# The last MLP's pair sums on DVE instead of POOL, and five slots instead of three for the weights of the modulation dot products

## The chip, the cores and the metric

The kernel runs on one core of a Trainium2 chip. The metric is the device time of one execution in microseconds (us). Five engines work side by side, each through its own instructions in order: PE (TensorE, matrix products), DVE (VectorE), ACT (ScalarE), POOL (GpSimd) and SP (SyncE, which here issues all DMA transfers). PE writes to PSUM, in banks of 128 x 512 f32 words; DVE and ACT read PSUM and SBUF, and POOL's instructions in this kernel read SBUF alone.

## The reference

Two layers of a diffusion backbone over 1024 latent tokens and 256 context tokens, 1024 channels wide: a convolution mixer with its MLP, then grouped-query attention with its MLP. Every sub-layer is modulated by vectors that come from a conditioning vector. What the change touches, cut down:

```python
sc = silu(c); scc = silu(c_ctx)
for i in range(2):
    mod_l = split(sc  @ w_mod[i] + b_mod[i], 6)       # 6 vectors of 1024
    mod_c = split(scc @ w_mod[i] + b_mod[i], 6)
    ...                                               # mixer: convolution (i = 0), attention (i = 1)
    hl = modulate(rms_norm(xl, norm2_g[i]), mod_l[3], mod_l[4])
    xl = xl + mod_l[5] * (square(relu(hl @ w_ff1[i])) @ w_ff2[i])     # d_ff = 4096
```

## The kernel before

All products are f32 made of three passes (high part times high, low times high, high times low), so each weight block is first split: ACT copies it to a rounded high part, and POOL or DVE subtracts to get the low part (`unit`, `lower`).

**The modulation vectors of layer 1** (`mods`, L338 to L370) are not made on PE. They are 128 dot products on DVE ("dots", L363): each takes a 128 x 512 block of weights (`rawh`, loaded by SP, L354) and multiplies it with half of silu(c) (`scp`, two PSUM banks written by ACT, L348, from the tile `sc`). They come in three runs (32 for c, 32 for c_ctx, 64 for c), each of which loads `sc` anew. The weights rotate through three slots, borrowed from the idle tiles `ks`, `vt`, `sb`, and a load is requested two dots ahead. The dots are background work: `pump` hands them out between the steps of layer 0's MLP (`mlp`), where each costs `MQ` credits. Their place on DVE, among the MLP's evacuations of PSUM (L439 `hb`, L461 `X`), is then set by a scheduler with its own idea of durations. In the trace they lie between 737 and 990 us.

**The last MLP** (`mlp1`) uses a seven-product scheme (Strassen-Winograd) on blocks. The loop over 16 pairs of hidden blocks (`for j in range(NP)`) makes, per pair, the products of S1 (bank b5), S3 (b7), S2 (b6), S4 (b5 again, added) and A22 (b7 again, added). For the first eight pairs (`pro`) the A11 product was made before and lies in DRAM (`p1d`), so a pair is five products; for the later ones it is seven. `w1_ops` prepares a pair's weights: SP loads `ra` and `rb` (L1343, L1344, three `raw` slots), DVE forms four sums in `work` (L1357 to L1361), ACT and POOL split them (L1350, L1198), and A22 is split by ACT and DVE (L1364, L1365) into the tile with the tag `p1`, which has one slot.

The sums of a pair: ACT copies b5 to p5 (L1409) and b7 to p7 (L1413), POOL adds p5 += p7 (L1416), DVE adds p1 += b6 (L1419), POOL adds p5 += p1 (L1420). `tail` runs one pair later: relu and square of p5 (`hidden`, L1307, L1308, with its store L1309), s12 = b5 + p1 and p1 = b7 + p1 on DVE (L1376, L1377), relu and square on ACT (L1378, L1379; L1307, L1308), the differences t1 (DVE L1384), t2 (POOL L1386), s12 (DVE L1388) and t4 (DVE L1391), each stored to `hd` by SP (L1383). S4 adds into b5, so PE cannot start S4 before the copy L1409 has read the bank. `ff2` then reads `hd`.

Of the kernel before, what the change touches and what calls it, by code (L numbers as in the profile page):

```python
# [14 lines left out]
AF = mybir.ActivationFunctionType  # L15
ALU = mybir.AluOpType
# [4 lines left out]
P = 128  # L21
D = 1024
KT = D // P
# [4 lines left out]
TAPS = 31  # L28
# [34 lines left out]
_off = 0  # L63
for _n, _w in [("n1", 16), ("n2", 16), ("bmod", 96), ("bdw", 8), ("lng", 8), ("lnb", 8), ("taps", 8 * TAPS)]:
    VEC[_n] = (_off, _w)
    _off += _w
# [12 lines left out]

MQ = 0.73  # L80
G3 = [4.2, 4.2, 4.2, 4.2]
# [31 lines left out]
BUFS = {"w8": 5, "raw": 3, "rawm": 1, "xu": 3, "hl": 2, "hb": 1, "tmp": 5, "acc": 3, "sc": 1, "qs": 1, "ks": 1,  # L113
        "vt": 1, "sb": 1, "cc": 1, "m3": 2, "halo": 1, "v4": 1, "r4s": 1, "r4y": 1, "pc": 10, "p1": 1}

# [12 lines left out]
class Kern:  # L128
# [209 lines left out]
    def mods(self, i1, chunks, cond, dst):  # L338
# [12 lines left out]
        def load(i):  # L351
            j, u, z = units[i]
            raw = self.t(("ks", "vt", "sb")[i % 3], [P, 512], "rawh")
            nc.sync.dma_start(out=raw, in_=self.A["wmod1"][j * 8 + u, :, z * 512:z * 512 + 512])  # L354
            return raw
        raws = [load(0), load(1)]
        for i, (j, u, z) in enumerate(units):
            if i + 2 < len(units):
                raws.append(load(i + 2))
            if u == z == 0:  # L360
                part = self.t("mp", [P, 2, 8], "mp")
            raw = raws.pop(0)
            nc.vector.tensor_tensor_reduce(raw, raw, scp[z], 1.0, 0.0, ALU.mult, ALU.add,  # L363
                                           accum_out=part[:, z, u:u + 1])
            yield MQ
            if u == 7 and z:
                nc.vector.tensor_tensor(part[:, 0], part[:, 0], part[:, 1], ALU.add)
                self.mod_done(i1, j, dst, part[:, 0])
                self.mdone.add((i1, cond, j))
                yield 0.2  # L370
# [160 lines left out]
    def conv_block(self, b):  # L531
# [5 lines left out]
        N -= off  # L537
        to, bo = VEC["taps"][0], VEC["bdw"][0]
        vs = None
        for c2 in range(0, KT, 2):  # L540
# [6 lines left out]
            for j in range(TAPS):  # L547
                for z in range(2):
                    ct = c2 + z
                    src = u[:, ct, off + j:off + j + N]  # L550
                    tap = self.vec[:, to + ct * TAPS + j:to + ct * TAPS + j + 1]
                    if j == 0:
# [647 lines left out]
    def mlp1(self, at, pre, r0):  # L1200
# [171 lines left out]
        def tail(j, p1, p5, s11, b5, b7):  # L1372
# [12 lines left out]
            out("T1", t1)  # L1385
            nc.gpsimd.tensor_tensor(t2, p5, t1, ALU.subtract)  # L1386
            out("T2", t2)
# [7 lines left out]
        for j in range(NP):  # L1395
# [3 lines left out]
            p1 = ring[2 * (j % 2)]  # L1399
            if pro:  # L1400
                nc.sync.dma_start(out=p1, in_=self.p1d[:, j])
            else:
                b1 = bank(q, "b1")
# [7 lines left out]
            self.prod(b7, u["S3"], piece("T3"), True)  # L1411
            p7 = self.t("acc", [P, 512], "p7")
            nc.scalar.activation(p7, b7, AF.Copy)  # L1413
            if last:
                tail(*last)
            nc.gpsimd.tensor_tensor(p5, p5, p7, ALU.add)  # L1416
            b6 = bank(q + 3, "b6")
            self.prod(b6, u["S2"], piece("T2"), True)
            nc.vector.tensor_tensor(p1, b6, p1, ALU.add)  # L1419
            nc.gpsimd.tensor_tensor(p5, p5, p1, ALU.add)  # L1420
            s11 = self.t("tmp", [P, 512], "s11")
# [118 lines left out]
    def build(self):  # L1540
# [3 lines left out]
        self.vec = const.tile([P, NVEC], F32, name="vec")  # L1544
        nc.sync.dma_start(out=self.vec, in_=self.A["vec"])
        self.ident = const.tile([P, P], F32, name="ident")
# [29 lines left out]
        self.pp = ctx.enter_context(tc.tile_pool(name="ps", bufs=1, space=PSUM))  # L1576

        self.halo = self.t("halo", [P, KT, HALO], "halo")
        self.hb = self.t("hb", [P, 8 * BW], "hb", F32R)
# [68 lines left out]
```

## Time and profile before

| | us |
|---|---|
| median of three runs (2904.96 to 2914.39) | 2907.84 |
| the profiled execution | 2907.84 |
| its span, first to last instruction | 2905.9 |
| PE busy in the span | 2752.6 (95%) |
| DVE, ACT, POOL busy | 2005.7, 1483.5, 1657.6 |

The span leaves 1.9 us of the execution's time around it. An engine's busy time counts only its computing instructions; a matmul's end is modelled, so a busy PE need not run at its peak. "Idle before, releaser" names the instruction whose end let a waiting engine go on.

### The profile page before, as it was taken

The page shows a single profiled execution, that of the slowest core. Times are in us where ns is not written, and L with a number is a line of the kernel's source. Part 1 is how long each engine was busy: PE and PEld are TensorE (multiplying, and loading weights), DVE is VectorE, ACT ScalarE, POOL GpSimd, SP SyncE. Part 2 cuts the span into 40 slices and gives each one's busy share as a digit, 9 for nine tenths or more (in the row PEclk, how much of TensorE's full clock was granted, in tenths as well). Part 3 has the DMA queues.
Part 4 walks back from the last instruction along what each step waited for, and adds up shares of the span by engine and source line. Part 5 has one row for each costly group of instructions (what it writes and reads, how often), then busy time and mean ns, then how long its engine had stood idle before and what let it go on. Part 6 is the DMA issues. An engine that isn't in the chain of part 4 may idle for free. (4 is left out here: it accounts for less than half of the span.)

```text
span 2905.9 us, 36468 instructions
## 1 busy us (share of the span) xinstructions
PE 2752.6 (95%) x12634; PEld 2314.2 (80%) x12634; DVE 2005.7 (69%) x3268; ACT 1483.5 (51%) x2386; POOL 1657.6 (57%) x1286
## 2 busy tenths in 40 slices
PE   7999999999988999989998899998999889999999
PEld 2778999999888999978886677776667677878887
DVE  3888988988465432456358899976986645458797
ACT  4543554546444354536345577655675544454332
POOL 3777766676565664444434466654666556564332
PEclk9999999999999999999999999999999999999999
DMA  6454433343776634444444411132106555474452
GB/s 240 167 176 153 132 120 109 116 141 119 266 239 202 206 109 160 132 133 129 138 145 142 133 22 23 22 95 65 23 8 208 160 181 170 148 254 174 160 176 103
DMA packets 176584, 406.69 MB, mean 140 GB/s; under 512 B 21328, under 2 KB 64848, under 8 KB 174352
## 3 DMA queue, kind: packets, MB, share of 16 engines
q1 hardware_dynamic: 176400, 404.37, 42.8%
q8 instruction: 99, 1.62, 0.2%
q14 instruction: 85, 0.70, 0.1%
HBM read 343.49 MB, written 60.82 MB: 139 GB/s over the span
## 5 line engine op out<-in xcount | busy, mean ns | idle before, releaser
L210 POOL TENSOR_TENSOR wsp<-raw,wsp 128x512 fp32r<-128x512 f32 x508 | 662.0, 1332 | 411.2 <-ACT wsp L207 370.2
L218 PE MATMUL ps<-h,wsp 128*128 128x432 f32 (+1 forms) x2832 | 575.9, 361 | 5.6 <-ACT h L318 2.3
L218 PEld LDWEIGHTS ps<-h,wsp 128*128 128x128 f32 x2832 | 534.8, 190 | 44.5 <-issue 8.3
L207 ACT ACTIVATE wsp<-raw 128x1024 fp32r<-128x1024 f32 x291 | 306.6, 1057 | 321.9 <-PE ps L218 208.0
L556 DVE SCALAR_TENSOR_TENSOR cv<-u,vec,cv 128x464 f32<-128x464 f32 (+2 forms) x696 | 423.1, 671 | 6.2 <-ACT cv L553 4.8
L218 PE MATMUL ps<-hb,wsp 128*128 128x432 f32 (+1 forms) x1920 | 399.3, 362 | 20.5 <-DVE X L461 12.6
L1083 POOL TENSOR_TENSOR p<-e,p 128x512 fp32r<-128x512 f32 x223 | 307.3, 1390 | 164.0 <-ACT p L1081 99.2
L218 PEld LDWEIGHTS ps<-hb,wsp 128*128 128x128 f32 x1920 | 363.3, 190 | 41.6 <-issue 16.3
L1188 PE MATMUL b<-u 128*128 128x512 f32 x1344 | 305.1, 389 | 1.0 <-DVE sums L1453 1.0
L1188 PEld LDWEIGHTS b<-u 128*128 128x128 f32 x1344 | 252.3, 188 | 53.7 <-issue 1.4
L1076 ACT ACTIVATE e<-sT 128x512 f32<-128x512 f32 x320 | 185.9, 596 | 122.0 <-PE sT L1074 100.6
L1038 DVE TENSOR_REDUCE m<-s 128x1 f32<-128x512 f32 (+1 forms) x336 | 191.9, 590 | 11.3 <-PE s L1036 10.1
L1198 POOL TENSOR_TENSOR u<-tf,u 128x512 fp32r<-128x512 f32 x56 | 101.5, 1833 | 150.3 <-ACT u L1447 136.1
L461 DVE SCALAR_TENSOR_TENSOR X<-ps,m,X 128x432 f32<-128x432 f32 (+2 forms) x144 | 81.3, 587 | 117.9 <-PE ps L218 117.7
L363 DVE CUSTOM_DVE_ANT_0 rawh<-rawh,scp 128x512 f32<-128x512 f32 x128 | 86.5, 685 | 108.2 <-DMA rawh<-in_wmod 101.1
L439 DVE TENSOR_TENSOR hb<-ps,hb 128x432 fp32r<-128x432 f32 (+1 forms) x96 | 57.5, 599 | 115.0 <-ACT ps L438 114.7
L1079 DVE CAST p<-e 128x512 fp32r<-128x512 f32 x160 | 115.5, 722 | 29.8 <-ACT e L1076 25.4
L1188 PE MATMUL b<-T,wsp 128*128 128x512 f32 x576 | 133.2, 389 | 0.0
L210 POOL TENSOR_TENSOR wx<-raw,wx 128x512 fp32r<-128x512 f32 x90 | 115.6, 1307 | 24.9 <-ACT wx L207 24.4
L1090 PE MATMUL O<-p,half 128*128 128x512 f32 x320 | 126.9, 396 | 0.0
L1188 PEld LDWEIGHTS b<-T,wsp 128*128 128x128 f32 x576 | 108.2, 188 | 22.6
L218 PE MATMUL ps<-h,wx 128*128 128x432 f32 (+1 forms) x624 | 125.5, 356 | 0.0
(314 smaller groups left out, 5346.5 us busy)
## 6 DMA issues: line engine op xcount, KB each, us to landing
raw<-in_w SPq DMA_DIRECT2D x232, 512.0 KB, 3.4
raw<-in_pw SPq DMA_DIRECT2D x72, 512.0 KB, 3.5
rawh<-in_wmod SPq DMA_DIRECT2D x128, 256.0 KB, 3.5
tf<-hd SPq DMA_DIRECT2D x56, 512.0 KB, 4.2
raw<-in_qkv SPq DMA_DIRECT2D x36, 512.0 KB, 3.4
rawp<-in_wmod SPq DMA_DIRECT2D x32, 512.0 KB, 4.3
raw<-in_w2s SPq DMA_DIRECT2D x16, 1024.0 KB, 7.0
hd<-t SPq DMA_DIRECT2D x48, 256.0 KB, 3.2
```

The source lines that it names most:

```text
L207: nc.scalar.activation(hi(c, n), raw[:, c * P:(c + n) * P], AF.Copy)
L210: (eng or nc.gpsimd).tensor_tensor(lo(c, n), raw[:, c * P:(c + n) * P], hi(c, n).bitcast(F32), ALU.subtract)
L218: self.nc.tensor.matmul(ps, lhsT=(wh, wl, wh)[t], rhs=(ah, ah, al)[t], start=first and i == t == 0, stop=last and i == n - 1 and t == 2)
L363: nc.vector.tensor_tensor_reduce(raw, raw, scp[z], 1.0, 0.0, ALU.mult, ALU.add, accum_out=part[:, z, u:u + 1])
L556: nc.vector.scalar_tensor_tensor(dst, src, tap, acc[z][:, :N], ALU.mult, ALU.add)
L1038: nc.vector.reduce_max(m3[:, qt, j, c:c + 1], s[:, :w], axis=AX.X)
L1076: nc.scalar.activation(e, s, AF.Exp, scale=0.125)
L1079: nc.vector.tensor_copy(p[:, 0], e)
L1083: (nc.vector if u % lm == lm - 1 else nc.gpsimd).tensor_tensor(p[:, 1], e, p[:, 0].bitcast(F32), ALU.subtract)
L1090: nc.tensor.matmul(O[1], lhsT=self.half, rhs=p[:, 0], start=a, stop=False)
L1188: self.nc.tensor.matmul(ps, lhsT=w[t % 2](k), rhs=(ah, ah, al)[t], start=first and k == t == 0, stop=k == 3 and t == 2, skip_group_check=True)
L1198: eng.tensor_tensor(w[:, 1, i:i + n], src[:, i:i + n], w[:, 0, i:i + n].bitcast(F32), ALU.subtract)
```

## The change

In the last MLP the second sum p5 += p7 is made by DVE straight from the bank b7, so that the copy to p7 goes; p5 += p1 and t2 move from POOL to DVE; the load of the stored product p1 is written after `tail`; the tag `p1` (A22's split) has two slots. In `mods` two more slots are taken from the halves of `sc`, a load is requested three dots ahead, and `MQ` goes from 0.73 to 1.2. The convolution's taps leave the tile `vec` for a tile of their own that is freed after the attention.

```diff
-        ... ("lnb", 8), ("taps", 8 * TAPS)]:
+        ... ("lnb", 8)]:
-MQ = 0.73
+MQ = 1.2
-        "vt": 1, "sb": 1, "cc": 1, "m3": 2, ... "pc": 10, "p1": 1}
+        "vt": 1, "sb": 1, "cc": 1, "taps": 1, "m3": 2, ... "pc": 10, "p1": 2}
...
         def load(i):
             j, u, z = units[i]
-            raw = self.t(("ks", "vt", "sb")[i % 3], [P, 512], "rawh")
+            if i % 5 < 3:
+                raw = self.t(("ks", "vt", "sb")[i % 5], [P, 512], "rawh")
+            else:
+                raw = sc[:, i % 5 * 512 - 1536:i % 5 * 512 - 1024]
             nc.sync.dma_start(out=raw, in_=self.A["wmod1"][j * 8 + u, :, z * 512:z * 512 + 512])
             return raw
-        raws = [load(0), load(1)]
+        raws = [load(i) for i in range(3)]
         for i, (j, u, z) in enumerate(units):
-            if i + 2 < len(units):
-                raws.append(load(i + 2))
+            if i + 3 < len(units):
+                raws.append(load(i + 3))
...
-            nc.gpsimd.tensor_tensor(t2, p5, t1, ALU.subtract)
+            nc.vector.tensor_tensor(t2, p5, t1, ALU.subtract)
...
-            if pro:
-                nc.sync.dma_start(out=p1, in_=self.p1d[:, j])
-            else:
+            if not pro:
                 b1 = bank(q, "b1")
...
-            p7 = self.t("acc", [P, 512], "p7")
-            nc.scalar.activation(p7, b7, AF.Copy)
+            nc.vector.tensor_tensor(p5, b7, p5, ALU.add)
             if last:
                 tail(*last)
-            nc.gpsimd.tensor_tensor(p5, p5, p7, ALU.add)
+            if pro:
+                nc.sync.dma_start(out=p1, in_=self.p1d[:, j])
             b6 = bank(q + 3, "b6")
             self.prod(b6, u["S2"], piece("T2"), True)
             nc.vector.tensor_tensor(p1, b6, p1, ALU.add)
-            nc.gpsimd.tensor_tensor(p5, p5, p1, ALU.add)
+            nc.vector.tensor_tensor(p5, p5, p1, ALU.add)
...
+        self.taps_w = self.t("taps", [P, KT * TAPS], "taps")
+        nc.sync.dma_start(out=self.taps_w, in_=self.A["vec"][:, NVEC:])
```

The lines of the changed kernel stand four lines later in `tail` and `w1_ops` (L1343 is L1347), and two later in the pair loop (L1409 is L1411, L1420 is L1422).

On DVE, one pair of the first eight before, from the first operand sum of the coming pair (names with a number are buffers; `raw` and `work` are as in the text above):

```order
L1357 TENSOR_TENSOR work<-raw 128x512
L1358 TENSOR_TENSOR work<-raw 128x512
L1360 TENSOR_TENSOR work<-work,raw 128x512
L1361 TENSOR_TENSOR work<-raw,work 128x512
L1419 TENSOR_TENSOR work<-b_20572,work 128x512
L1376 TENSOR_TENSOR s_20665<-b_20520,work 128x512
L1384 TENSOR_TENSOR t_20673<-s_20665,s_20587 128x512
L1388 TENSOR_TENSOR s_20665<-work,s_20665 128x512
L1377 TENSOR_TENSOR work<-b_20534,work 128x512
L1365 TENSOR_TENSOR a_20629<-raw,a_20629 128x512
L1391 TENSOR_TENSOR t_20681<-work,t_20674 128x512
```

The same engine and a pair of the first eight, of the changed kernel, from its second row on:

```order
L1362 TENSOR_TENSOR work<-raw 128x512
L1414 TENSOR_TENSOR work<-b_20821,work 128x512
L1364 TENSOR_TENSOR work<-work,raw 128x512
L1365 TENSOR_TENSOR work<-raw,work 128x512
L1421 TENSOR_TENSOR work<-b_20858,work 128x512
L1422 TENSOR_TENSOR work<-work 128x512
L1380 TENSOR_TENSOR s_20949<-b_20807,work 128x512
L1388 TENSOR_TENSOR t_20957<-s_20949,s_20873 128x512
L1381 TENSOR_TENSOR work<-b_20821,work 128x512
L1369 TENSOR_TENSOR a_21026<-raw,a_21026 128x512
L1390 TENSOR_TENSOR t_20958<-work,t_20957 128x512
L1392 TENSOR_TENSOR s_20949<-work,s_20949 128x512
```

Three rows are new: the sum with b7 (L1414) behind the coming pair's first two operand sums, p5 += p1 (L1422) directly behind p1 += b6, and t2 (L1390).

On SP, the same pair before, with the two weight loads `raw` of coming pairs and the stores to `hd` of p5, t1, t2, s12, p1 and t4:

```order
L1343 DMA raw<-in_w 128x1024
L1309 DMA hd<-work 128x512
L1383 DMA hd<-t_20786 128x512
L1383 DMA hd<-t_20787 128x512
L1383 DMA hd<-s_20778 128x512
L1344 DMA raw<-in_w 128x1024
L1309 DMA hd<-work 128x512
L1383 DMA hd<-t_20794 128x512
L1423 DMA s_20813<-hd 128x512
L1401 DMA work<-p1d 128x512
```

And of the changed kernel:

```order
L1347 DMA raw<-in_w 128x1024
L1313 DMA hd<-work 128x512
L1387 DMA hd<-t_20846 128x512
L1348 DMA raw<-in_w 128x1024
L1313 DMA hd<-work 128x512
L1387 DMA hd<-t_20847 128x512
L1387 DMA hd<-s_20838 128x512
L1387 DMA hd<-t_20854 128x512
L1425 DMA s_20873<-hd 128x512
L1418 DMA work<-p1d 128x512
```

The second weight load stood behind the stores of t1, t2 and s12 and now stands directly behind that of t1; the load of the stored product has kept its place in the queue.

On SP, in the first stretch of the dots before: `raw` (L197) are the MLP's weights, `rawh` the dots' weights, and `sc` here is the conditioning vector of the second run.

```order
L197 DMA raw<-in_w 128x1024 x2
L354 DMA rawh<-in_wmod 128x512 x2
L197 DMA raw<-in_w 128x1024
L354 DMA rawh<-in_wmod 128x512 x3
L197 DMA raw<-in_w 128x1024
L354 DMA rawh<-in_wmod 128x512 x3
L342 DMA sc<-in_cctx 128x1024
L354 DMA rawh<-in_wmod 128x512 x7
L197 DMA raw<-in_w 128x1024
```

The same place of the changed kernel, where `sc<-in_wmod` are the dots' weights in the two new slots:

```order
L197 DMA raw<-in_w 128x1024 x2
L358 DMA sc<-in_wmod 128x512 x2
L197 DMA raw<-in_w 128x1024
L358 DMA rawh<-in_wmod 128x512 x3
L197 DMA raw<-in_w 128x1024
L358 DMA sc<-in_wmod 128x512 x2
L358 DMA rawh<-in_wmod 128x512 x3
L358 DMA sc<-in_wmod 128x512 x2
L358 DMA rawh<-in_wmod 128x512 x3
L358 DMA sc<-in_wmod 128x512 x2
L358 DMA rawh<-in_wmod 128x512 x2
L197 DMA raw<-in_w 128x1024
```

Between the last two weight loads of these pieces stood ten loads for dots and the second run's `sc`, and now stand fourteen loads and no `sc`.

Further on in the same queue of the changed kernel, the second run's `sc` comes:

```order
L358 DMA sc<-in_wmod 128x512 x2
L358 DMA rawh<-in_wmod 128x512
L197 DMA raw<-in_w 128x1024
L358 DMA rawh<-in_wmod 128x512
L342 DMA sc<-in_cctx 128x1024
L358 DMA rawh<-in_wmod 128x512
L197 DMA raw<-in_w 128x1024
```

It has moved behind the last two dots of the first run that use `sc` as slots, so it can only be issued when they are done; two of ACT's L348 stand right behind, on ACT ahead of the next evacuation.

## Rows read from the trace of the kernel before

**Rows 1.** The head of the page, and its first part: busy us, share of the span and instructions of each engine.

```profile
span 2905.9 us, 36468 instructions
PE 2752.6 (95%) x12634; PEld 2314.2 (80%) x12634; DVE 2005.7 (69%) x3268; ACT 1483.5 (51%) x2386; POOL 1657.6 (57%) x1286
```

**Rows 2.** Busy time in three stretches: the dots (737 to 990 us), the first eight pairs (2307.97 to 2440.70) and the later eight. Columns: stretch, its length, busy us (instructions) of PE, PEld (weight loads), DVE, ACT and POOL, then the granted TensorE clock as a share of full speed, the DMA engines' busy share, GB/s.

```profile
737.00:990.00 253.00, 227.66 (x1098) 210.78 (x1097) 140.05 (x378) 110.37 (x184) 146.01 (x119) 0.97 0.71 234
2307.97:2440.70 132.73, 117.04 (x481) 93.05 (x480) 64.72 (x84) 59.98 (x90) 83.16 (x61) 0.96 0.55 182
2440.70:2594.00 153.30, 152.47 (x665) 124.59 (x664) 75.44 (x87) 80.73 (x123) 98.24 (x70) 1.00 0.52 170
```

**Rows 3.** Waits of PE between 2290 and 2620 us: what waited, for whom, us in total, times, the longest.

```profile
PE b L1188 <- ACT work L1409: 15.6, 7, 3.2
PE b L1188 <- ACT work L1405: 0.8, 2, 0.6
```

**Rows 4.** PE in order of time in the pair loop (start, us, operation, in brackets the idle time before it and its releaser). The rows with T and x36 are the products of S1, S3 and S2 of one pair; the row with u,wsp is S4.

```profile
2307.97 8.32 PE L1188 MATMUL b<-T,wsp 128*128 128x512 f32 x36
...
2322.13 8.32 PE L1188 MATMUL b<-T,wsp 128*128 128x512 f32 x36
2333.32 4.54 PE L1188 MATMUL b<-u,wsp 128*128 128x512 f32 x12 [2.86 <-ACT work L1409]
...
2440.70 2.88 PE L1188 MATMUL b<-B,wsp 128*128 128x512 f32 x12
```

**Rows 5.** All engines in order of time over one pair of the first eight.

```profile
2323.01 2.63 POOL L1198 TENSOR_TENSOR wsp<-work,wsp 128x512 fp32r<-128x512 f32 x2 [1.73 <-ACT wsp L1350]
2323.16 0.69 DVE L1419 TENSOR_TENSOR work<-b,work 128x512 f32<-128x512 f32 x1
...
2325.60 1.29 POOL L1420 TENSOR_TENSOR work<-work 128x512 f32<-128x512 f32 x1
...
2326.93 0.63 ACT L1307 ACTIVATE work<-work 128x512 f32<-128x512 f32 x1 [2.59 <-POOL work L1420]
...
2329.44 0.69 DVE L1384 TENSOR_TENSOR t<-s,s 128x512 f32<-128x512 f32 x1 [4.81 <-ACT s L1379]
...
2330.21 1.77 POOL L1386 TENSOR_TENSOR t<-work,t 128x512 f32<-128x512 f32 x1 [0.80 <-DVE t L1384]
2330.77 0.68 DVE L1377 TENSOR_TENSOR work<-b,work 128x512 f32<-128x512 f32 x1
...
2332.68 0.58 ACT L1409 ACTIVATE work<-b 128x512 f32<-128x512 f32 x1
...
2332.89 0.40 SPq L1344 DMA_DIRECT2D raw<-in_w  x1
...
2337.80 0.69 DVE L1357 TENSOR_TENSOR work<-raw 128x512 f32<-128x512 f32 x1 [4.24 <-DMA raw<-in_w]
2338.41 0.69 DVE L1358 TENSOR_TENSOR work<-raw 128x512 f32<-128x512 f32 x1
...
2339.13 1.06 ACT L1350 ACTIVATE wsp<-work 128x1024 fp32r<-128x1024 f32 x1 [5.38 <-DVE work L1358]
...
2350.11 0.40 SPq L1344 DMA_DIRECT2D raw<-in_w  x1
```

**Rows 6.** Groups of instructions by line between 2308 and 2600 us, of DVE (two SBUF inputs) and of ACT: busy us and mean ns of one, then idle us before them and releasers.

```profile
L1388 DVE TENSOR_TENSOR s<-work,s 128x512 f32<-128x512 f32 x15 | 20.1, 1340 | 0.2
L1307 ACT ACTIVATE work<-work 128x512 f32<-128x512 f32 x31 | 19.6, 632 | 105.7 <-POOL work L1420 87.0 <-DVE work L1377 18.7
```

**Rows 7.** Waits of PE between 700 and 1050 us.

```profile
PE ps L218 <- DVE X L461: 12.6, 7, 3.5
PE ps L218 <- DVE hb L439: 7.1, 6, 3.0
PE st L253 <- DVE acc L286: 5.6, 1, 5.6
```

**Rows 8.** The tile `rawh`: the dots on DVE (ns min/median/max), what ended DVE's idle time before them (us, times), and the time from a load's issue to its landing.

```profile
L363 DVE CUSTOM_DVE_ANT_0 rawh<-rawh,scp x128: 671/686/691, 737.8 to 990.1; 128x512 f32<-128x512 f32 x128
...
  DMA rawh<-in_wmod: 101.1, 67
...
DMA to landing us min/median/max: 2.5/3.5/7.4
```

**Rows 9.** Moments of the dots' stretch: a dot and the evacuation behind it on DVE, then PE; and PE at half clock behind its longest wait.

```profile
757.48 0.69 DVE L363 CUSTOM_DVE_ANT_0 rawh<-rawh,scp 128x512 f32<-128x512 f32 x1 [1.70 <-DMA rawh<-in_wmod]
...
759.99 0.40 DVE L461 SCALAR_TENSOR_TENSOR X<-ps,m,X 128x176 f32<-128x176 f32 x1
...
760.92 1.41 PE L218 MATMUL ps<-hb,wsp 128*128 128x432 f32 x3 [3.54 <-DVE X L461]
...
875.32 5.31 PE L218 MATMUL ps<-h,wsp 128*128 128x432 f32 x14
```

**Rows 10.** The loads of `sc` between 735 and 990 us (KB each, us from issue to landing), and what ACT waited for before its L348 (us, times).

```profile
sc<-in_cctx SPq DMA_DIRECT2D x1, 512.0 KB, 6.0
sc<-in_c SPq DMA_DIRECT2D x1, 512.0 KB, 4.6
...
  DVE mp L363: 8.9, 3
```

**Rows 11.** SP's second issue after the start.

```profile
1.18 0.42 SPq L632 DMA_DIRECT2D cc<-in_ccol  x1
```

More of the change, by code (lines that the diff above doesn't have):

```diff
@@ L63 @@
 _off = 0
-for _n, _w in [("n1", 16), ("n2", 16), ("bmod", 96), ("bdw", 8), ("lng", 8), ("lnb", 8), ("taps", 8 * TAPS)]:
+for _n, _w in [("n1", 16), ("n2", 16), ("bmod", 96), ("bdw", 8), ("lng", 8), ("lnb", 8)]:
     VEC[_n] = (_off, _w)
@@ L113 @@
 BUFS = {"w8": 5, "raw": 3, "rawm": 1, "xu": 3, "hl": 2, "hb": 1, "tmp": 5, "acc": 3, "sc": 1, "qs": 1, "ks": 1,
-        "vt": 1, "sb": 1, "cc": 1, "m3": 2, "halo": 1, "v4": 1, "r4s": 1, "r4y": 1, "pc": 10, "p1": 1}
+        "vt": 1, "sb": 1, "cc": 1, "taps": 1, "m3": 2, "halo": 1, "v4": 1, "r4s": 1, "r4y": 1, "pc": 10, "p1": 2}
 KEEP = ("w8", "raw", "xu", "tmp", "acc", "v4", "r4s", "r4y")
@@ L537, in conv_block @@
         N -= off
-        to, bo = VEC["taps"][0], VEC["bdw"][0]
+        bo = VEC["bdw"][0]
         vs = None
@@ L550, in conv_block @@
                     src = u[:, ct, off + j:off + j + N]
-                    tap = self.vec[:, to + ct * TAPS + j:to + ct * TAPS + j + 1]
+                    tap = self.taps_w[:, ct * TAPS + j:ct * TAPS + j + 1]
                     if j == 0:
@@ L1544, in build @@
         self.vec = const.tile([P, NVEC], F32, name="vec")
-        nc.sync.dma_start(out=self.vec, in_=self.A["vec"])
+        nc.sync.dma_start(out=self.vec, in_=self.A["vec"][:, 0:NVEC])
         self.ident = const.tile([P, P], F32, name="ident")
```

## The prediction

> **What bounds the kernel now.** The page's first part shows PE busy for 2752.6 of 2905.9 us [rows 1]: the kernel is a string of matmuls, and an edit on DVE, ACT or POOL is worth what it takes from PE's waits, about 153 us over the whole span. So I read where PE waits in the stretches that the edits touch [rows 2]. In the later eight pairs PE is busy for 152.47 of 153.30 us: nothing is to be had there. In the first eight pairs it is busy for 117.04 of 132.73, and in the stretch of the dots for 227.66 of 253.00. These two are the whole prize.
>
> **The pair loop, before.** The first pair runs without a wait: from its S1 to the next pair's S1 is 2322.13 - 2307.97 = 14.16 us [rows 4]. Eight such pairs are 113.3 us; they take 2440.70 - 2307.97 = 132.73, or 16.6 each. The loss is 19.45 us. The waits of PE put down to the copy of b5 (L1409) are 15.6 of it [rows 3]. The other 3.85 are matmuls behind such a wait: S4 took 4.54 us after a wait of 2.86 [rows 4], and the granted clock is 0.96 in this stretch against 1.00 in the next [rows 2], so part of it ran at 1.2 instead of 2.4 GHz.
>
> Why is the copy late? One pair in order of time [rows 5] shows a chain that goes round once per pair. DVE adds p1 at 2323.16, but POOL is in two splits of 2.63 us and adds p5 only from 2325.60 to 2326.89. ACT had waited 2.59 us for it, and over the stage it waited 87.0 us for this line [rows 6]. ACT's relu and squares follow, DVE makes t1 at 2329.44, POOL takes 1.77 us for t2, and SP, which stores t1, t2 and s12 in order, issues the weight load L1344 at 2332.89. The weights let DVE go on at 2337.80, 4.91 us later. The next L1344 is at 2350.11: the circle is 17.2 us, longer than PE's 14.16. The copy L1409 at 2332.68 hangs on it through ACT's order.
>
> **The change there, step by step.**
> - p5 += p1 goes from POOL to DVE, directly behind p1 += b6. DVE's instructions start 0.61 us apart and take 0.69 [rows 5], so the sum ends at about 2323.16 + 0.61 + 0.69 = 2324.5 instead of 2326.9: 2.4 us taken from the circle.
> - t2 on DVE is 0.69 instead of 1.77, and the load L1344 no longer stands behind its store: another 2 us. The copy to p7 leaves ACT; p5 += b7 is one more instruction on DVE. The read of a bank is an operation that the trace has: 0.69 for L1419 [rows 5].
> - The new circle: load 4.91, seven DVE starts from L1357 to p5 += p1 (6 x 0.61 + 0.69 = 4.35), then ACT from L1307 to DVE's t1, 2.51 before (2329.44 - 2326.93) and one split of 1.06 more that now stands between, then t1 itself and its store's issue, 0.69 + 0.40. That is 13.9 us, just under 14.16. PE becomes the bound of the loop.
> - Does PE then wait for L1409? A22, the pair's last product, ends as the next pair starts. DVE's p1 += b7 takes 0.7, two ACT steps 1.3, and the copy follows S1 (a third of 8.32, 2.8): done at 3.4 us, while S4 starts at 8.3. There are 5 us to spare, which also cover a circle that runs a little over.
> - DVE gets 3 x 0.69 = 2.1 us per pair, 81 us in all on a stretch of 113: hidden by its idle time. If the cover were gone it would be 16 us. POOL loses three sums per pair, two of them of 1.29 and 1.77 us [rows 5].
> - The second slot for A22 lets its split run before PE has read the last one; the later place of the p1 load is needed only by p1 += b6, 8 us into the pair. Both at nothing, hidden behind PE; without the cover a late p1 would cost up to the 3.5 us that a load of its size takes to land [rows 8], once per pair.
>
> So 19.45 and the 0.8 of the later pairs [rows 3] come into reach. I keep 2 us for the first round, in which the order is not yet the steady one, and take 18.2. Bounds: 20.2 if all goes, 10 if half of it does.
>
> **The dots, before.** A dot takes 0.686 us, and before 67 of the 128 DVE stood idle for the weights, 101.1 us in all [rows 8]: 1.48 us a dot. Three slots explain this: issue 0.4, landing 3.5, dot 0.69 is 4.6 us for three dots, 1.53 each. DVE works in order, so an evacuation behind a waiting dot is late: a dot waits 1.70 us until 757.48, the evacuation starts at 759.99, and PE has lost 3.54 us [rows 9]. PE lost 25.3 us this way (12.6 + 7.1 + 5.6) [rows 7]. To it comes half clock: 0.97 over 253 us [rows 2] is 7.6 us of clock; of the pairs' 0.04 x 132.73 = 5.3 us, 3.85 showed as loss, and the same share here is 5.5. At stake: 30.8 us.
>
> **The change there.** With five slots the ring gives a dot every 4.6 / 5 = 0.92 us. The new order asks for more, too: in the piece shown fourteen loads stand where ten stood, so at the old pace a dot has 1.48 / 1.4 = 1.06 us. That is still above 0.92, so most of the waits should go, in spite of the denser dots, and the last dots are through earlier. I leave the 5.6 us wait for the sum of squares as it is, with its half clock (14 matmuls in 5.31 us [rows 9], some 2.6 over): that is a chain of ACT and DVE steps with the dots between. Of the other 22.6 I take three quarters, 17.
>
> Against it stands the new order of `sc`. The vector of the second and third run can only be loaded when the last dots of the run before have left its halves: issue 0.4, landing 5.3 (6.0 and 4.6 [rows 10]), and two ACT steps of 0.6 (L1409, of the same size, took 0.58 [rows 5]) make 6.9 us, in which ACT stands in front of the MLP's evacuations. Before, ACT waited 8.9 / 3 = 3.0 us there [rows 10]. Twice 3.9 more is 7.8; some of it is covered by banks already evacuated, so I take 6. Net gain 11; bounds from a loss of 8 (nothing regained) to a gain of 22.6.
>
> The taps' own load puts one SP issue, 0.42 us [rows 11], ahead of the first weights: 0.4 lost, at most; nothing if it is hidden. `MQ` acts only through the order above.
>
> **Sum.** The profiled execution took 2907.84 us, 1.9 of it around the span, and equals the median of the runs shown. 2907.84 - 18.2 - 11 + 0.4 = 2879.
>
> **Rivals.**
> - *The dots gain nothing.* More dots stand ahead of each evacuation, and 0.69 us each they fill the time that the waits leave; for it speaks that the 5.6 us wait is such a place, against it that 0.92 is under 1.06. Then 2907.84 - 18.2 + 0.4 = 2890.
> - *The reload of `sc` eats the gain.* Both reloads reach PE whole, 6.9 us and some 1.5 of half clock each: 17, as much as was regained. Also 2890. For it: ACT's order. Against it: PE has several banks.
> - *The circle ends at about 15.3 us*, because loads land later than 4.9 us. Then 8 x 1.1 = 9 us of the pairs' loss stay: 2888.
> - *DVE becomes the bound of the pairs, and the kernel slower.* L1388, with both inputs in SBUF, took 1340 ns in the mean where 0.69 is its length [rows 5, 6]: it ran into POOL's work. If all six such instructions of the new circle did (each 0.65 more), the circle would be 13.9 + 3.9 = 17.8 us, over the 16.6 of now, and no slack would last eight pairs: 8 x 1.2 = 10 slower. With no gain from the dots that is 2918. It decides from a circle of 16.6 on. Against it: POOL gives up its three sums. The Trainium skill (SBUF — State Buffer, Who interferes with whom) states that a DVE instruction with two SBUF inputs and a GpSimd instruction that reads SBUF block each other for a whole instruction; the trace's 1340 ns agrees with it. By that rule each sum moved to DVE is exposed to POOL's splits, which speaks for this rival.
>
> **How the numbers follow.** The forecast has 0.55 and gives 2868 to 2889; the dots without gain 0.15; the reload 0.12; the longer circle 0.14; the slower case 0.04. The range of 2866 to 2896 takes in the first four with their bounds: 2865 if both stages gave all, 2896 if the pairs gave 12 and the dots nothing. 0.3%, 8.7 us, is about what a measurement can tell from no change. Faster than 2899: the forecast and nearly all of the next three, 0.90; within 0.3%: 0.07; slower: 0.03.
>
> **What would show it.** Right: PE's waits for the b5 copy shrink from 15.6 us to under 3; pairs of 14.2 us; the granted clock of that stretch at 0.99 or more; DVE's wait for the dots' weights well below 101 us; PE's waits for `X` and `hb` about halved; two ACT waits for the load of `sc` of 3 to 6 us. Wrong: DVE's two-input sums stretched to 1.3 us with pairs of 16 us; PE's waits in the dots' stretch still 25 us.

## The result and the profile after

The changed kernel takes 2879.86 us (median of four, 2876.51 to 2884.47) beside 2908.98 for the kernel before on the same chip: a ratio of 0.991, 95% interval 0.9895 to 0.9925. The forecast was 2879.0. The total agrees, but hardly any term of the sum does.

The head of the page and its first part, after [rows 1]:

```profile
span 2879.5 us, 36460 instructions
PE 2737.8 (95%) x12634; PEld 2310.6 (80%) x12634; DVE 2022.5 (70%) x3312; ACT 1474.9 (51%) x2370; POOL 1602.5 (56%) x1246
```

Two stretches after, columns as in [rows 2]: one that holds all the dots (its bounds are given below), and the first eight pairs.

```profile
665.70:1038.90 373.20, 350.13 (x1752) 331.80 (x1751) 196.40 (x476) 174.24 (x288) 229.49 (x185) 0.98 0.61 205
2292.25:2417.11 124.86, 114.32 (x481) 90.64 (x480) 82.52 (x112) 59.46 (x89) 57.68 (x41) 0.99 0.61 206
```

The eight pairs fell from 132.73 to 124.86 us; eight at 14.16 would be 113.3. What PE still waits for in them, after [rows 3]:

```profile
PE b L1192 <- DVE work L1414: 6.0, 5, 1.8
PE b L1192 <- ACT work L1411: 4.5, 4, 2.1
```

The copy of b5 (L1411, before L1409) cost 15.6 us and now costs 4.5; a wait that the forecast did not have, for DVE's read of b7 (L1414), costs 6.0. The circle after, in order of time, as in [rows 5]: the load L1348, which was L1344, to the next one.

```profile
2332.01 0.33 SPq L1348 DMA_DIRECT2D raw<-in_w  x1
2332.12 0.58 ACT L1411 ACTIVATE work<-b 128x512 f32<-128x512 f32 x1
...
2336.26 0.69 DVE L1361 TENSOR_TENSOR work<-raw 128x512 f32<-128x512 f32 x1 [2.46 <-POOL wsp L1202]
2336.86 0.69 DVE L1414 TENSOR_TENSOR work<-b,work 128x512 f32<-128x512 f32 x1
...
2337.60 3.08 PE L1192 MATMUL b<-u,a 128*128 128x512 f32 x12 [1.79 <-DVE work L1414]
...
2345.10 0.32 SPq L1387 DMA_DIRECT2D hd<-t  x1
2345.60 1.19 DVE L1369 TENSOR_TENSOR a<-raw,a 128x512 fp32r<-128x512 f32 x1
...
2346.81 0.33 SPq L1348 DMA_DIRECT2D raw<-in_w  x1
```

It is 14.80 us long, not 13.9. The load does not go at the store of t1 (2345.10): it waits for a raw slot, which comes free when DVE has split A22 (L1369, done at 2346.79). Among SP's own waits in the eight pairs this one stands five times:

```profile
SPq L1348 <- DVE a L1369: 7.1, 5, 1.8
```

A22's products add into b7, so PE cannot start them before L1414 has read that bank, and L1414 stands on DVE behind L1361, which waits for the weights and for a place in `work`. In the round shown POOL's split (L1202) was the last to release it; over the eight pairs the weights were so seven times (16.5 us) and POOL twice (4.9 us). The rows stand below, beside the fourth place for weights.

The dots after [rows 8], first those in the old slots, then in the same view of the tile `sc` the idle time before those in its halves:

```profile
L367 DVE CUSTOM_DVE_ANT_0 rawh<-rawh,scp x79: 671/686/691, 729.3 to 932.3; 128x512 f32<-128x512 f32 x79
...
  DMA rawh<-in_wmod: 37.8, 27
...
DMA to landing us min/median/max: 2.5/4.4/7.5
```

```profile
  DMA sc<-in_wmod: 19.7, 13
```

DVE's waits for dot weights fell from 101.1 to 37.8 + 19.7 = 57.5 us, but PE's waits in the dots' stretch hardly fell: 22.9 us instead of 25.3 [rows 7], close to the 25 that the forecast named as a sign of being wrong.

```profile
PE ps L218 <- DVE hb L443: 9.9, 6, 3.6
PE st L253 <- DVE acc L286: 7.6, 1, 7.6
PE ps L218 <- DVE X L465: 5.4, 4, 2.8
```

`X` fell from 12.6 to 5.4, as forecast or better; `hb`, which was to be halved too, rose by 2.8 and the sum of squares by 2.0.

**Where the time went.** The same five moments of PE can be found in every run: the start of the broadcast of a row's statistics (tile `rb`) for the fifth, the seventh and the ninth time (381.5, 675.0 and 1054.7 us in the first profile of before; called the fifth, seventh and ninth sum below), the first S1 of the loop (2307.97) and the first product of the ninth pair (2440.70). Each run's length between them, in us, with the granted clock from 120 to 195 us:

| run | to the fifth | clock | seventh to ninth (dots) | eight pairs | after them |
|---|---|---|---|---|---|
| before | 381.5 | 0.95 | 379.7 | 132.7 | 465.2 |
| before again | 376.7 | 0.95 | 382.1 | 135.6 | 462.5 |
| taps alone | 379.9 | 0.93 | 380.0 | 133.5 | 462.7 |
| slot and taps alone | 378.2 | 0.93 | 379.7 | 134.8 | 471.7 |
| dots alone | 378.1 | 0.95 | 376.9 | 134.2 | 462.5 |
| pairs alone | 380.9 | 0.93 | 378.8 | 122.2 | 462.5 |
| pairs, slot, taps | 373.4 | 1.00 | 380.2 | 125.4 | 462.5 |
| the change | 373.0 | 1.00 | 373.2 | 124.9 | 462.4 |
| the change again | 371.7 | 1.00 | 373.2 | 125.3 | 462.4 |
| no slot, no taps | 374.9 | 0.98 | 375.2 | 123.1 | 462.5 |
| b7 copied by ACT | 369.9 | 1.00 | 374.1 | 126.1 | 462.4 |
| fourth place | 381.2 | 0.95 | 373.8 | 122.3 | 462.4 |
| fourth place later | 383.5 | 0.95 | 373.5 | 121.6 | 462.5 |
| no reload | 377.7 | 0.95 | 373.4 | 124.8 | 462.6 |

Of the 26.4 us between the two first profiles, the start gave 8.5, the dots 6.5, the eight pairs 7.9 and the rest of the program 2.8; 0.7 are left for the two stretches not shown. The experiments below show that only the dots and the pairs come from edits.

A profile is one execution, and two things in these show how far one moves. From the ninth sum to the first S1 no edit acts, and yet this stretch takes from 1252.0 us (b7 copied by ACT) to 1259.7 (dots alone). PE is idle for 78.4 to 81.7 us of it in all 14 profiles; what differs is how long the matmuls take, as the rows of these two runs show (columns as in [rows 2]):

```profile
1036.70:2288.67 1251.97, 1170.37 (x5258) 951.58 (x5256) 848.60 (x1381) 723.21 (x1277) 689.73 (x528) 0.99 0.33 102
1048.50:2308.21 1259.71, 1181.17 (x5258) 958.62 (x5258) 847.94 (x1381) 722.49 (x1275) 688.43 (x528) 0.98 0.34 101
```

And the profiled execution need not be a typical one. That of the ACT copy was the fastest of its six (2878.95 us, median 2887.4); those of the dots alone and of the two runs with a fourth place were the slowest of theirs (2906.71, 2886.77 and 2888.67).

### The profile page after: what moved, and what is told of

The parts are those of the page before. It is cut to its first block, busy times and chain, and to the rows that moved or that the text cites. A ratio compares the mean times of both kernels' runs of the same rounds, so it can differ in the third digit from the quotient of the medians.

```text
span 2879.5 us, 36460 instructions
## 1 busy us (share of the span) xinstructions
PE 2737.8 (95%) x12634; PEld 2310.6 (80%) x12634; DVE 2022.5 (70%) x3312; ACT 1474.9 (51%) x2370; POOL 1602.5 (56%) x1246
## 5 line engine op out<-in xcount | busy, mean ns | idle before, releaser
L210 POOL TENSOR_TENSOR wsp<-raw,wsp 128x512 fp32r<-128x512 f32 x514 | 669.9, 1331 | 384.6 <-ACT wsp L207 342.9
L560 DVE SCALAR_TENSOR_TENSOR cv<-u,taps,cv 128x464 f32<-128x464 f32 (+2 forms) x696 | 422.9, 670 | 3.7 <-ACT cv L557 2.1
L1202 POOL TENSOR_TENSOR u<-tf,u 128x512 fp32r<-128x512 f32 x56 | 102.8, 1856 | 169.9 <-ACT u L1449 156.9
L443 DVE TENSOR_TENSOR hb<-ps,hb 128x432 fp32r<-128x432 f32 (+1 forms) x96 | 57.5, 599 | 137.7 <-ACT ps L442 137.5
L1202 POOL TENSOR_TENSOR wsp<-work,wsp 128x512 fp32r<-128x512 f32 x64 | 91.8, 1456 | 104.8 <-ACT wsp L1354 96.4
```

The costliest lines, as they stand in the source:

```text
L210: (eng or nc.gpsimd).tensor_tensor(lo(c, n), raw[:, c * P:(c + n) * P], hi(c, n).bitcast(F32), ALU.subtract)
L560: nc.vector.scalar_tensor_tensor(dst, src, tap, acc[z][:, :N], ALU.mult, ALU.add)
L1202: eng.tensor_tensor(w[:, 1, i:i + n], src[:, i:i + n], w[:, 0, i:i + n].bitcast(F32), ALU.subtract)
```

## The experiments

Ratios are to runs of the kernel before on the same chip, with a 95% interval. "Eight pairs" runs to the first product of the ninth, as in the table; the expectations of the runs with the fourth place later, without slot and taps, and with these alone count to the start of the last A22, by which the changed kernel has 121.8 us.

**The parts alone.** The taps' own tile:

```diff
-    nc.sync.dma_start(out=self.vec, in_=self.A["vec"])
+    nc.sync.dma_start(out=self.vec, in_=self.A["vec"][:, 0:NVEC])
...
+    nc.sync.dma_start(out=self.taps_w, in_=self.A["vec"][:, NVEC:])
```

> The kernel before with one edit alone: the convolution's taps in a tile of their own, loaded by a DMA behind that of the vectors. In the trace of the changed kernel 8.6 us were already gained by the time 371 us, in a stretch where the order of all instructions is the same as before. Theory A: the taps' own tile and load bring that gain: about 2900 us, and the sum-of-squares matmuls at 371.7 us come at about 363. Theory B: the early gain belongs to something else (execution to execution, or the layout of the tiles that the other edits move): 2908 within 3 us, and 0.4 us lost at the start.

Measured: 2904.14 us, 0.999 (0.9976 to 1.0004). This cannot be told from no change, and the start took 379.9 us, nearer to theory B.

The edits in `mods` (`MQ`, five slots, three loads ahead):

```diff
-MQ = 0.73
+MQ = 1.2
...
-            raw = self.t(("ks", "vt", "sb")[i % 3], [P, 512], "rawh")
+            if i % 5 < 3:
+                raw = self.t(("ks", "vt", "sb")[i % 5], [P, 512], "rawh")
+            else:
+                raw = sc[:, i % 5 * 512 - 1536:i % 5 * 512 - 1024]
...
-        raws = [load(0), load(1)]
+        raws = [load(i) for i in range(3)]
...
```

> The kernel before with the edits to the dot products alone (five slots, three ahead, MQ 1.2). From the trace of the changed kernel the stretch from 675 to 1042 us was 6.4 us shorter. Theory A: the parts add: 6.4 us of gain, about 2902. Theory B: the early gain comes with this edit, through other places of tiles: about 2894. If the dots are worth the 11 us that were forecast: 2898 with no early gain.

Measured: 2900.53 us, 0.9983 (0.9972 to 0.9994). The dots' stretch gave about 3 us here, and 6.5 in the runs of the whole change.

The pair loop's edits with one slot for A22:

```diff
-            nc.scalar.activation(p7, b7, AF.Copy)
+            nc.vector.tensor_tensor(p5, b7, p5, ALU.add)
...
-            nc.gpsimd.tensor_tensor(p5, p5, p1, ALU.add)
+            nc.vector.tensor_tensor(p5, p5, p1, ALU.add)
```

> The kernel before with the edits to the pair loop alone, without the second slot for A22's split. From the trace of the changed kernel the first eight pairs were 7.9 us shorter and what follows 2.8 us. Theory A: 10.7 us of gain, about 2898; PE waits for A22 on the DVE sum with b7 as in the changed kernel (6 us). Theory B: the second slot is what the loop needs: without it the pairs stay at 16 us and the gain is under 4 us. The forecast's step (PE alone bounds the pairs) would give 2889.

Measured: 2895.46 us, 0.9964 (0.9949 to 0.9979). This is 10.6 us under the 2906.07 of before beside it, as theory A had it. The eight pairs take 122.2 us: the pair edits give the loop's whole gain without the second slot.

**The kernel before, once more**, with no edit:

> The kernel before, unchanged, for a second profile: how far do the same places of the program move between executions? Theory A (the early gain is the taps'): the matmuls at 371.7 us come within 1 us of there. Theory B (execution to execution): they move by several us with no edit at all. Time 2908 within 3.

Measured: 2904.31 us, 0.9999 (0.9986 to 1.0012). Without an edit its profile reaches the fifth sum 4.8 us earlier than the first one did. So the start moves by itself.

**The change, once more:**

> The changed kernel once more, beside the kernel before. If the 29 us are the change's, the ratio comes out within 0.989 to 0.993 again. The two stretches that belong to an edit should repeat within 2 us: the first eight pairs of the last MLP (124.9 us in its first profile, against 132.7 before) and the dot-product stretch. The start (to 371 us), in which the first profile gained 8.6 us with hardly an edit in it, need not repeat: if that gain belongs to the execution, it comes out anywhere between 0 and 9 us; if it belongs to the moved taps, at 7 to 9 us again.

Measured: 2884.11 us beside 2903.88, 0.9932 (0.9912 to 0.9952). Its pairs and dots repeat within 0.5 us.

**The second slot for A22.** First the pair edits with slot and taps:

```diff
-... "pc": 10, "p1": 1}
+... "taps": 1, ... "pc": 10, "p1": 2}
```

> The pair loop's edits with the second slot for a22 (and the taps' tile, without which the slot does not fit); the dot products as before. It differs from the run of the pair edits alone (0.9964 of before) by the second slot and by the taps' tile, which alone gave 0.999. Theory one, the second slot lets a pair's products begin ahead of the pair before it: 8 us more than the pair edits alone, about 2887 us (0.994), and the first eight pairs at 125 us. Theory two, the slot is worth nothing, because the pairs wait for the raw loads and for DVE either way: about 2895 us (0.9965), and the first eight pairs as long as in the run of the pair edits alone.

Measured: 2889.72 us, 0.9951 (0.9935 to 0.9968). The eight pairs take 125.4 us, 3.2 more than with one slot. Theory one has its total nearly, and its reason is wrong: the gain lies at the start, where the clock was 1.00.

Then the whole change with one slot and the taps in `vec`:

> The changed kernel without the second slot for a22 and without the taps' tile: dot products and pair loop as in the change. Theory one, slot and taps are worth nothing or less: the first eight pairs take 119 us, as in the run of the pair edits alone, instead of 121.8, the start has no part in it, and the time is that of the changed kernel or up to 3 us less, 2879 to 2883. Theory two, the placement that comes with slot and taps is worth 5 us at the start: the fifth sum of squares at 376 to 382 us, and a time of 2885 to 2889.

Measured: 2890.23 us, 0.9947 (0.9932 to 0.9963). The loop is shorter again (123.1, or 118.6 by the count of the expectation), and yet the time is not that of theory one. Theory two nearly has the time, but not the place: the start took 374.9 us. Beside the first profile of the change this one is 8.5 us longer: 2.0 at the start, 2.0 in the dots' stretch, 5.5 between the ninth sum and the first S1, where no edit acts, and 0.8 elsewhere, less 1.8 in the pairs. In the 5.5 it is the matmuls that take longer, as above; why they do is open.

Last, the kernel before with slot and taps alone:

> The kernel before with only the taps' tile and the second slot for a22, so with all that decides where tiles lie in SBUF as in the changed kernel, and with none of the moved sums and dot products. So far four of five profiles with both of these reach the fifth sum of squares at 370 to 373 us and have the full granted clock from 120 to 195 us; none of five without both does (376 to 382 us, clock 0.93 to 0.95). Theory one, the placement (or the smaller first load) makes the start faster: 370 to 374 us, clock 1.00 from 120 to 195, and a ratio of about 0.998. Theory two, the start belongs to the execution: either of the two, and a ratio of 1.000 within 0.0015. The second slot by itself should leave the first eight pairs at 130 to 133 us, since there the wait for the b5 copy sets their pace.

Measured: 2913.15 us, 1.0031 (1.0019 to 1.0043). Neither theory has this time, and the start took 378.2 us. The start from 120 to 195 us, in this run, in the changed kernel, and in the changed kernel with the fourth place used later (below), one row each:

```profile
120.00:195.00 75.00, 68.28 (x321) 55.38 (x318) 66.62 (x118) 34.10 (x47) 57.85 (x52) 0.93 0.51 174
```

```profile
120.00:195.00 75.00, 72.48 (x359) 59.07 (x358) 67.99 (x129) 40.40 (x56) 62.76 (x57) 1.00 0.54 184
```

```profile
120.00:195.00 75.00, 68.16 (x328) 55.08 (x327) 66.40 (x116) 32.00 (x43) 56.11 (x51) 0.95 0.49 166
```

The first and the last have slot and taps and do not have the full clock. Placement therefore does not bring the fast start by itself. Four of eight profiles with slot and taps have it and none of six without (the nearest has 0.98); whether it moves the odds stays open. The run shows another thing: in the loop of before, the second slot costs 9 us behind the first eight pairs (471.7 against 462.7 with the taps alone; the medians differ by 9.2), part of it in the later pairs, where PE was busy for 152.47 of 153.30 us [rows 2] and now is not.

```profile
2442.27:2595.27 153.00, 147.51 (x634) 119.62 (x633) 71.67 (x79) 72.93 (x114) 90.80 (x66) 0.99 0.44 149
```

**What paces the pairs.** ACT copies b7 again, and DVE adds the copy:

```diff
-            nc.vector.tensor_tensor(p5, b7, p5, ALU.add)
+            p7 = self.t("acc", [P, 512], "p7")
+            nc.scalar.activation(p7, b7, AF.Copy)
+            nc.vector.tensor_tensor(p5, p5, p7, ALU.add)
```

> The changed kernel, but the seventh product is copied from PSUM by ACT again and DVE adds the copy: A22's products then wait for an ACT copy that ends early and no longer for DVE's read. Theory one, the pairs are paced by the circle of the raw loads (14.8 us a pair: DVE splits a22, its raw slot comes free, the load is issued and lands, DVE goes on), and the wait for L1414 is only where it shows: the wait moves to other products, the first eight pairs stay at 123 to 126 us, and the time within 3 us of the changed kernel. Theory two, the wait for DVE's read is itself the loss: the 6.0 us of waits for L1414 and part of the 4.5 us for L1411 go, the first eight pairs take 115 to 118 us, and the time falls by 6 to 9 us.

Measured: 2887.4 us, 0.9938 (0.992 to 0.9957), eight pairs 126.1 us. PE's waits in the eight pairs of this run:

```profile
PE b L1192 <- ACT work L1411: 10.9, 7, 3.7
```

Of 6.0 + 4.5 us of waits 10.9 are left, all at the b5 copy, and the load L1348 goes round as before, here in 15.05 us:

```profile
2345.01 0.33 SPq L1348 DMA_DIRECT2D raw<-in_w  x1
...
2360.06 0.33 SPq L1348 DMA_DIRECT2D raw<-in_w  x1
```

Theory one holds in what it says of the wait for L1414: it shows a circle and does not make it.

A fourth place for raw weights, made of two tiles of the ring `acc`, so that a load can be issued a pair ahead:

```diff
-                ra, rb = [self.t("raw", [P, 1024], "raw") for _ in range(2)]
+                ra = self.t("raw", [P, 1024], "raw")
+                if j % 2:
+                    r0, r1 = [self.t("acc", [P, 512], "rawb") for _ in range(2)]
+                else:
+                    rb = self.t("raw", [P, 1024], "raw")
...
```

> The changed kernel with a fourth place for raw weights in the pair loop (in every second pair the second operand goes to two slots of a ring that the loop does not use, by two loads of half the size), so that a load is issued a pair ahead and not when DVE has just split the piece before it. Theory one, the circle of the raw loads sets 14.8 us a pair: the waits for L1414 go with it, a pair falls to its products' 14.2 us, the first eight pairs take 114 to 118 us, and the time falls by 7 to 11 us below the changed kernel's. Theory two, DVE's order sets it (L1414 behind the tail of the pair before): nothing changes, 123 to 126 us and a time within 3 us of the changed kernel.

Measured: 2880.59 us, 0.9924 (0.9906 to 0.9941), eight pairs 122.3 us: the first two 18.53 and 17.74 (14.83 and 16.79 in the changed kernel), the other six 86.1 against 93.2. The time is 3.5 us under that of the change beside it (2884.11), within the noise, and the pairs lie between the two theories. DVE's waits in the changed kernel (2292 to 2417 us), and then with the fourth place (2296 to 2425):

```profile
DVE work L1361 <- DMA raw<-in_w: 16.5, 7, 3.9
DVE t L1388 <- ACT s L1383: 12.4, 5, 2.9
DVE work L1361 <- POOL wsp L1202: 4.9, 2, 2.5
DVE work L1364 <- POOL wsp L1202: 3.1, 1, 3.1
```

```profile
DVE work L1370 <- POOL wsp L1202: 15.7, 6, 3.1
DVE work L1373 <- POOL wsp L1202: 6.7, 6, 3.1
DVE t L1397 <- ACT s L1392: 4.3, 2, 2.9
```

The wait for weights is gone, and in its place the same instruction (L1361, here L1370) waits for POOL: the operand sums have one set of places in `work`, and POOL must have read the last set.

So the load is not alone in pacing the pairs. Of the eight, the middle four (the fourth to the seventh) take 57.0 us with the fourth place and 58.9 without, and 58.4 in the next run. There L1370 comes round every 14.87 us, each time released by POOL:

```profile
2355.38 1.76 DVE L1370 TENSOR_TENSOR work<-rawb 128x512 f32<-128x512 f32 x1 [3.10 <-POOL wsp L1202]
...
2370.25 1.77 DVE L1370 TENSOR_TENSOR work<-raw 128x512 f32<-128x512 f32 x1 [3.09 <-POOL wsp L1202]
```

A second circle, through POOL's splits and the places in `work`, is about as long as that of the load (14.80), and shows once the load is out of the way.

The same from the third pair on (`if j and j % 2 == 0` instead of `if j % 2`):

> The changed kernel with the fourth place for raw weights used in every second pair from the third pair on; the first two pairs load as in the changed kernel. In the first run with a fourth place the first two pairs took 18.5 and 17.7 us (14.8 and 16.8 in the changed kernel) and the other six 83.2 (90.2). Theory one, the raw loads' circle paces the loop from the third pair on, and the two long pairs came of operands that had to wait for the ring that the stage before still used: 14.8, 16.8 and 83 to 85, in all 114 to 117 us against 121.8, and a time 5 to 8 us below the changed kernel's. Theory two, the six short pairs only gave back what the first two had lost (work that had run ahead in the meantime): 120 to 123 us, and the time of the changed kernel within 3 us.

Measured: 2882.36 us, 0.9926 (0.991 to 0.9941), eight pairs 121.6 us (118.8 by the count of the expectation, again between the two theories): 19.75 for the first, and 101.8 for the other seven against 110.0. The first pair in order of time:

```profile
2308.90 13.16 POOL L1202 TENSOR_TENSOR wsp<-work,wsp 128x512 fp32r<-128x512 f32 x8 [1.72 <-ACT wsp L1363]
...
2310.73 1.75 DVE L1370 TENSOR_TENSOR work<-rawb 128x512 f32<-128x512 f32 x1 [1.19 <-POOL wsp L1202]
...
2312.41 1.77 DVE L1371 TENSOR_TENSOR work<-raw,rawb 128x512 f32<-128x512 f32 x1
2314.10 1.76 DVE L1373 TENSOR_TENSOR work<-work,raw 128x512 f32<-128x512 f32 x1
2315.97 1.57 DVE L1374 TENSOR_TENSOR work<-raw,work 128x512 f32<-128x512 f32 x1
2317.45 0.68 DVE L1423 TENSOR_TENSOR work<-b,work 128x512 f32<-128x512 f32 x1
...
2318.19 4.61 PE L1192 MATMUL b<-u,a 128*128 128x512 f32 x12 [3.66 <-DVE work L1423]
```

With the weights there early, four sums of the coming pair stand ahead of the read of b7 (L1423), each at 1.57 to 1.77 us instead of 0.68 beside eight POOL splits in a row. PE waits 3.66 us, and A22 then takes 4.61 us instead of 2.97, at a granted clock of 0.63. Neither version with a fourth place can be told from the change.

**The price of the reload.** `sc` is loaded once. The kernel leaves out the second and third load and four of ACT's six silu steps, so the context's modulation is made from the wrong vector:

```diff
+        if not self.kept:
             nc.sync.dma_start(out=sc, in_=self.A[cond].broadcast_to([P, D]))
...
+        if self.kept:
+            scp = self.kept
...
```

> The changed kernel, but the conditioning vector is loaded and passed through silu once, for the first run of dot products; the second run, which needs the context's vector, uses the first one's. This leaves out the second and third loads of sc and four ACT steps, and the layer-1 modulation of the context is computed from the wrong vector. Theory one, the reload eats the gain (ACT waited 13.4 and 8.6 us for these loads in the changed kernel): the stretch from 675 to 1055 us of the kernel before, which takes 373.2 us in the changed kernel and 380.2 before, falls to 362 to 368, and the time by 6 to 11 us. Theory two, the reload is hidden by the banks already evacuated and the gain is small because the weights land later (4.4 to 4.6 us instead of 3.5): 371 to 374 us, and a time within 3 us of the changed kernel.

Measured: 2883.98 us, 0.9925 (0.991 to 0.9941); the dots' stretch 373.4 us against 373.2. Theory two holds: no cost of the reload is seen, though ACT waits 8.6 and 7.5 us for the two reloads in the changed kernel (the 13.4 us of the expectation hold a wait for the first load, too):

```profile
780.30 1.12 ACT L348 ACTIVATE scp<-sc 128x512 f32<-128x512 f32 x2 [8.64 <-DMA sc<-in_cctx]
...
829.50 1.12 ACT L348 ACTIVATE scp<-sc 128x512 f32<-128x512 f32 x2 [7.50 <-DMA sc<-in_c]
```

## Why the total was right and its terms were not

**Pairs: 18.2 us forecast, 9.0 measured** (mean of the four runs with before's loop and one slot, 134.0, to the change's three with its loop unaltered, 125.0). The mechanism was right: the b5 copy's wait shrank, the clock rose from 0.96 to 0.99, DVE's load was hidden (82.5 us; 81 forecast). Four steps failed.
- *The circle.* 13.9 forecast, 14.8 measured, over PE's 14.16. The load was taken to follow t1's store; it follows DVE's split of A22, 1.7 us later. By its size this is the rival of the longer circle, with 9 us of the loss left, but not by its reason: the loads did not land later (2332.01 to L1361 at 2336.26 is 4.25 us, 4.91 before).
- *"A22, the pair's last product, ends as the next pair starts", and only the b5 copy was looked at.* A22 adds into b7, and the change gave the reading of b7 to DVE: 6.0 us of PE's waits. The run with ACT's copy shows that they are the circle's loss at another place, not a further one.
- *"5 us to spare" for the copy.* It was put at 3.4 us into the pair and ran at 2332.12 in a pair that began at 2323.87, 8.25 into it: on ACT it stands behind the squares, and so behind the circle.
- *"2 us for the first round".* Over 14.16 us each, the first three pairs lost 5.8 (14.83, 16.79, 16.65), the next four 2.2, and the last 3.6: 11.6 in all. The steady pairs were nearly right at 14.7. But 14.16 is not PE's least: the seventh pair after took 13.82 (2385.56 to 2399.38), and the first pair of before 13.78 in its second profile, so each pair had 0.4 us more to give than the forecast saw.

The trace of before had a sign of the first step: there A22's split was done at 2332.52, only 0.37 us ahead of the load (2332.89 [rows 5]).

```profile
2331.37 1.15 DVE L1365 TENSOR_TENSOR a<-raw,a 128x512 fp32r<-128x512 f32 x1
```

The second slot was put at nothing and costs 2 to 3 us here: 125.4 with it against 122.2 in the pair edits, and 125.0 against 123.1 in the whole change, with one profile each on the side without it. How it costs them is open.

The rival of the stretched sums is there in part. Of the three sums moved to DVE only p5 += p1 and t2 have both inputs in SBUF; p5 += b7 (L1414) reads a bank. In the changed kernel an operand sum from SBUF is stretched (L1362), L1414 is not:

```profile
L1362 DVE TENSOR_TENSOR work<-raw 128x512 f32<-128x512 f32 x10 | 10.1, 1012 | 0.0
L1414 DVE TENSOR_TENSOR work<-b,work 128x512 f32<-128x512 f32 x8 | 5.5, 684 | 1.9 <-ACT work L1411 1.9
```

**Dots: 17 regained and 6 lost forecast, so 11; measured 6.5 regained** (380.1 in six runs without these edits, 373.5 in the six with them and the taps' tile; 376.9 and 375.2 in the two with them and the taps in `vec`) **and nothing lost.** The ring's step used a landing of 3.5 us; with more loads in flight it is 4.4, so by the same sum the ring gives a dot every (0.4 + 4.4 + 0.69) / 5 = 1.10 us, no longer under the 1.06 asked for. But the larger error is to turn DVE's waits into PE's: 43.6 us of DVE's went and 2.4 of PE's, because the waits for `hb` and for the sum of squares grew, as the first rival had it; that the denser dots ahead of them are the reason is likely and not shown by itself. The rest of the 6.5 is in shorter matmuls, at a granted clock of 0.98 in both, and what shortened them is open: PE's busy time over the stretch fell by 4.2 us, to 350.13 from this row of before:

```profile
675.00:1054.70 379.70, 354.36 (x1752) 332.90 (x1751) 197.66 (x476) 174.08 (x288) 229.15 (x185) 0.98 0.61 202
```

The reload was priced by ACT's wait; the run without it shows no cost in the stretch (373.4 against 373.2 us). That banks already evacuated cover it, as the forecast had it for a part, is the likely reason. The price was misread, too: the 8.9 us before were three waits for two reloads, 4.5 each and not 3.0.

**The rest.** The two terms are too large by 9.2 and 4.5 us, 13.7 together. In the first profiles the start's 8.5 and the end's 2.8 filled most of that gap: the total came out by luck. The second comparison gives 19.8 us where 29 were forecast. The 0.4 us for the taps' load cannot be seen in a start that moves by itself. The start is not the edits': all of them are in the two runs that reach the fifth sum at 381.2 and 383.5 us. The end's 2.8 is the first profile of before, since 462.4 to 462.7 us stand in every other run but that of slot and taps. The traced edits are worth 9.0 + 6.5 = 15.5 us, the medians say 29.1 and, in the second comparison, 19.8. Some 4 to 14 us are thus attributed to no edit, and the runs do not settle whether the slower pieces of the runs without slot and taps belong to them.

## What to carry over

When an instruction that frees a PSUM bank moves to another engine, look at every product that adds into that bank and at what stands ahead of the instruction in its new queue. A circle's length is set by the last of all the things its load waits for, a slot's release too, and its run-in and run-out are to be counted pair by pair. Look for a second circle of the same length before paying for the shortening of the first: here the weights and POOL's splits paced the pairs together. Before a total that fits is taken as a proof, compare the same moments in several profiles: here the start, with the same code in both, took 369.9 and 383.5 us.

## What was not expected of the hardware

DVE's sum of two SBUF operands, 0.68 us alone, took 1.57 to 1.77 beside POOL's splits, and the one with an input in a bank (L1423) 0.68 in the same row of splits. The Trainium skill (SBUF — State Buffer, Who interferes with whom) says that a DVE instruction with two SBUF inputs and a GpSimd one that reads SBUF block each other for a whole instruction; the trace agrees. The forecast had it as the rival that makes the kernel slower; it came in part in the changed kernel (1012 ns in the mean for L1362) and most where the weights were early. A 256 KB load landed after 4.4 us in the median instead of 3.5 with five slots in use.
